# An RMSNorm and swish kernel: row loads and stores regrouped, the first stores held back, and some row sums moved to ScalarE

## The chip, the cores and the metric

The kernel runs on one core of one Trainium2 chip. The metric is the device time of one execution in microseconds (us), as the median of several runs. Slow runs, over 1.5% above the fastest of the same kernel, are left out. A *span* is the stretch that the profile covers in one execution; the time is about 1.3 us longer (160.02 us against 158.7 us in the profiled run of the kernel before). "Row" means a row in each of 128 partitions: 512 floats, 2 KB in a partition, 0.262 MB in all. The kernel moves 128 such rows in and 128 out. A *piece* is the part of one transfer that belongs to one partition: a load of 16 rows has 128 pieces of 32 KB.

## The reference

```python
def reference(x, gamma, eps):            # x: 16 x 1024 x 512 float32
    rms = np.sqrt(np.mean(x ** 2, axis=-1, keepdims=True) + eps)
    x_norm = x / rms * gamma
    return (x_norm * (1.0 / (1.0 + np.exp(-x_norm)))).astype(np.float32)
```

## The kernel before

The rows go through the core in 32 units of 4. For unit k, ScalarE squares and sums one row by itself (its accumulator) and squares the other three into PSUM; VectorE sums those three; GpSimd makes 1/rms; VectorE multiplies the four rows by it and by gamma, in place; ScalarE applies the swish, in place. SyncE issues the loads, ScalarE's queue the stores. The buffer is a ring of 96 rows, so the last 32 rows are loaded only when the first 32 have been stored.

```python
    sizes = [4, 4, 8] + [16] * 6 + [8, 8]     # rows of one load, and of one store
    ring = 96
    cn = 4                                    # rows of a unit
    n_sq = 3                                  # rows of a unit that VectorE sums
    ...
    def load(t):
        ...                                   # waits for the stores that free its part of the ring
        return nc.sync.dma_start(out=buf(t), in_=dram(xf, t)).then_inc(ld[t], 16)
    ...
    def square(k):
        t, at, first = chunks[k]
        if first:
            nc.scalar.wait_ge(ld[t], 16)
        acc = nc.scalar.activation(
            out=junk[k % 2], in_=xb[:, at + n_sq, :], func=AF.Square,
            scale=inv_d**0.5, accum_out=ms[:, k, n_sq : n_sq + 1],
        )
        ...
        square = nc.scalar.activation(
            out=sq[k % 2][:, 0:n_sq, :], in_=xb[:, at : at + n_sq, :],
            func=AF.Square, scale=inv_d**0.5,
        )
    ...
    for k in range(K + 3):
        if k < K:
            square(k)
        while stored < T and ends[stored] <= k - 2:
            store(stored)
            stored += 1
        if 2 <= k < K + 2:
            swish(k - 2)
```

Of the kernel before, what the change touches and what calls it, by code (L numbers as in the profile page):

```python
# [8 lines left out]
@with_exitstack  # L9
def kernel(  # L10
    ctx: ExitStack,
    tc: tile.TileContext,
    x: bass.AP,
    gamma: bass.AP,
    eps: bass.AP,
    out: bass.AP,
):
    nc = tc.nc
    P = nc.NUM_PARTITIONS
    AF = mybir.ActivationFunctionType  # L20
    ALU = mybir.AluOpType
    fp32 = mybir.dt.float32
    bf16 = mybir.dt.bfloat16

    xf = x.flatten_outer_dims()
    of = out.flatten_outer_dims()
    R, D = xf.shape


    sizes = [4, 4, 8] + [16] * 6 + [8, 8]  # L30
    ring = 96
    early = 2
    cn = 4
    n_sq = 3
    N = sum(sizes)
    assert N * P == R, (N, R)


    tiles = []
    done = 0  # L40
    for sz in sizes:
        assert done % ring + sz <= ring
        tiles.append((done * P, sz, done % ring))
        done += sz
    T = len(tiles)

    chunks = [
        (t, r, r == at)
        for t, (_, sz, at) in enumerate(tiles)
        for r in range(at, at + sz, cn)  # L50
    ]
    K = len(chunks)
    ends = []
    e = 0
    for sz in sizes:
        e += sz // cn
        ends.append(e)

    inv_d = 1.0 / float(D)
    eps_f = float(eps)  # L60



    tc.close()
    tc.compile()  # L65

    def sbuf(name, shape, dt=fp32):
        return nc.alloc_sbuf_tensor(name, shape, dt).ap()

    xb = sbuf("xb", [P, ring, D])  # L70
    gamma4 = sbuf("gamma4", [P, D])
    gamma_sb = sbuf("gamma_sb", [P, D])
    junk = [sbuf(f"junk{i}", [P, D], bf16) for i in range(2)]
    neg_half = sbuf("neg_half", [P, cn])
    ms = sbuf("ms", [P, K, cn])
    aeps = sbuf("aeps", [P, K, cn])
    rstd = sbuf("rstd", [P, K, cn])
    sq = [nc.alloc_psum_tensor(f"sq{i}", [P, 4, D], fp32).ap() for i in range(2)]

    ld = [nc.alloc_semaphore(f"ld{t}") for t in range(T)]  # L80
    st = [nc.alloc_semaphore(f"st{t}") for t in range(T)]
    scratch = nc.dram_tensor("scratch", [P, 16], fp32, kind="Internal").ap()
    blank = sbuf("blank", [P, 16])
    s_blank = nc.alloc_semaphore("s_blank")
    s_scratch = nc.alloc_semaphore("s_scratch")
    s_gld = nc.alloc_semaphore("s_gld")
    s_zero = nc.alloc_semaphore("s_zero")
    s_half = nc.alloc_semaphore("s_half")
    s_gamma = nc.alloc_semaphore("s_gamma")
    s_acc = nc.alloc_semaphore("s_acc")  # L90
    s_sq = nc.alloc_semaphore("s_sq")
    s_sum = nc.alloc_semaphore("s_sum")
    s_eps = nc.alloc_semaphore("s_eps")
    s_rstd = nc.alloc_semaphore("s_rstd")
    s_norm = nc.alloc_semaphore("s_norm")
    s_swish = nc.alloc_semaphore("s_swish")

    def need(ins, sem, value):
        return ins.wait_op(sem, value, "sem-ge")

    def dram(ap, t):
        first, sz, _ = tiles[t]
        return ap[first : first + P * sz].rearrange("(p n) d -> p n d", n=sz)

    def buf(t):
        _, sz, at = tiles[t]
        return xb[:, at : at + sz, :]


    stored_by_sync = set()  # L110

    def load(t):
        _, sz, at = tiles[t]
        waits = [
            u for u in range(t)
            if tiles[u][2] < at + sz and at < tiles[u][2] + tiles[u][1]
            and u not in stored_by_sync
        ]
        for u in waits:
            nc.sync.wait_ge(st[u], 16)  # L120
            stored_by_sync.add(u)
        return nc.sync.dma_start(out=buf(t), in_=dram(xf, t)).then_inc(ld[t], 16)

    entry = nc.main_func.blocks[0].instructions
    here = nc.cur_bb.bb.instructions
    for t in range(early):
        ins = load(t).ins
        assert here[-1] is ins or here[-1].name == ins.name
        here.pop()
        at = next(  # L130
            i for i, other in enumerate(entry)
            if other.engine == mybir.EngineType.SP
            and isinstance(other, mybir.InstDrain)
        )
        entry.insert(at, ins)
    for t in range(early, T):
        load(t)
    nc.sync.wait_ge(s_scratch, 16)


    nc.gpsimd.memset(blank, 0.0).then_inc(s_blank, 1)  # L141
    nc.gpsimd.memset(gamma4, 0.0).then_inc(s_zero, 1)  # L142
    nc.gpsimd.memset(neg_half, -0.5).then_inc(s_half, 1)  # L143
    nc.gpsimd.wait_ge(s_half, 1)
    for k in range(K):
        need(
            nc.gpsimd.tensor_scalar(  # L147
                out=aeps[:, k, :], in0=ms[:, k, :], scalar1=eps_f, scalar2=None,
                op0=ALU.add,
            ),  # L150
            s_sum, k + 1,
        ).then_inc(s_eps, 1)
        need(
            nc.gpsimd.tensor_tensor(  # L154
                out=rstd[:, k, :], in0=aeps[:, k, :], in1=neg_half, op=ALU.pow
            ),
            s_eps, k + 1,
        ).then_inc(s_rstd, 1)


    def square(k):
        t, at, first = chunks[k]
        if first:
            nc.scalar.wait_ge(ld[t], 16)
        acc = nc.scalar.activation(  # L165
            out=junk[k % 2], in_=xb[:, at + n_sq, :], func=AF.Square,
            scale=inv_d**0.5, accum_out=ms[:, k, n_sq : n_sq + 1],
        )
        if k >= 2:
            need(acc, s_acc, k - 1)  # L170
        acc.then_inc(s_acc, 1)
        square = nc.scalar.activation(  # L172
            out=sq[k % 2][:, 0:n_sq, :], in_=xb[:, at : at + n_sq, :],
            func=AF.Square, scale=inv_d**0.5,
        )
        if k >= 2:
            need(square, s_sum, k - 1)
        square.then_inc(s_sq, 1)

    def swish(k):  # L180
        _, at, _ = chunks[k]
        rows = xb[:, at : at + cn, :]
        need(
            nc.scalar.activation(out=rows, in_=rows, func=AF.Silu), s_norm, k + 1  # L184
        ).then_inc(s_swish, 1)

    def store(t):
        need(
            nc.scalar.dma_start(out=dram(of, t), in_=buf(t)), s_swish, ends[t]
        ).then_inc(st[t], 16)  # L190

    need(nc.scalar.dma_start(out=scratch, in_=blank), s_blank, 1).then_inc(
        s_scratch, 16
    )
    need(
        nc.scalar.dma_start(out=gamma4[0:P:32, :], in_=gamma.partition_broadcast(4)),
        s_zero, 1,
    ).then_inc(s_gld, 16)
    nc.scalar.preload_act_table_set("silu_and_others")  # L199
    stored = 0  # L200
    for k in range(K + 3):
        if k < K:
            square(k)
        while stored < T and ends[stored] <= k - 2:
            store(stored)
            stored += 1
        if 2 <= k < K + 2:
            swish(k - 2)


    def sums(k):
        need(
            nc.vector.tensor_reduce(  # L213
                out=ms[:, k, 0:n_sq], in_=sq[k % 2][:, 0:n_sq, :], op=ALU.add,
                axis=mybir.AxisListType.X,
            ),
            s_sq, k + 1,
        ).then_inc(s_sum, 1)

    def norm(k):  # L220
        _, at, _ = chunks[k]
        for j in range(cn):
            row = xb[:, at + j, :]
            ins = nc.vector.scalar_tensor_tensor(  # L224
                out=row, in0=row, scalar=rstd[:, k, j : j + 1], in1=gamma_sb,
                op0=ALU.mult, op1=ALU.mult,
            )
            if j == 0:
                need(ins, s_rstd, k + 1)
        ins.then_inc(s_norm, 1)  # L230

    for k in range(K + 1):
        if k < K:
            sums(k)
        if k == 0:
            need(
                nc.vector.stream_shuffle(gamma_sb, gamma4, [0] * 32), s_gld, 16  # L237
            ).then_inc(s_gamma, 1)
        if k == 1:
            nc.vector.wait_ge(s_gamma, 1)  # L240
        if k >= 1:
            norm(k - 1)


    for t in range(T):
        if t not in stored_by_sync:
            nc.sync.wait_ge(st[t], 16)

# [34 lines left out]
```

## Time and profile before

| | kernel before |
|---|---|
| time | 160.11 us, median of 3 (159.87 to 160.23) |
| busy: VectorE, ScalarE, GpSimd | 87%, 79%, 41% of the span |
| the 16 DMA engines | 99.2% of the span, 67.15 MB, 423 GB/s |
| last store: issued, landed | 150.1 us, 158.7 us |

These lines of the groups (shapes kept apart) are the ones that the change touches; the columns are line, engine, operation, output and input, count, then busy us and mean ns of one, then the idle time before them:

```profile
L213 DVE TENSOR_REDUCE ms<-sq 128x3 f32<-128x1536 f32 x32 | 56.1, 1754 | 7.0 <-ACT sq L172 7.0
L172 ACT ACTIVATE sq<-xb 128x1536 f32<-128x1536 f32 x32 | 45.9, 1433 | 0.0
L165 ACT ACTIVATE junk<-xb 128x512 bf16<-128x512 f32 x32 | 19.7, 615 | 3.4 <-DMA xb<-in_x_dram 3.3
```

A row sum on VectorE is at most a third of 1754 ns (585 ns); on ScalarE it is an operation of its own of 615 ns.

### The profile page before, as it was taken

The page shows a single profiled execution, that of the slowest core. Times are in us where ns is not written, and L with a number is a line of the kernel's source. Part 1 is how long each engine was busy: PE and PEld are TensorE (multiplying, and loading weights), DVE is VectorE, ACT ScalarE, POOL GpSimd, SP SyncE. Part 2 cuts the span into 40 slices and gives each one's busy share as a digit, 9 for nine tenths or more (in the row PEclk, how much of TensorE's full clock was granted, in tenths as well). Part 3 has the DMA queues.
Part 4 walks back from the last instruction along what each step waited for, and adds up shares of the span by engine and source line. Part 5 has one row for each costly group of instructions (what it writes and reads, how often), then busy time and mean ns, then how long its engine had stood idle before and what let it go on. Part 6 is the DMA issues. An engine that isn't in the chain of part 4 may idle for free.

```text
span 158.7 us, 439 instructions
## 1 busy us (share of the span) xinstructions
DVE 138.9 (87%) x162; ACT 125.3 (79%) x129; POOL 65.4 (41%) x71
## 2 busy tenths in 40 slices
DVE  0249999999999999999999999999999999999300
ACT  0935989888888889988888888888998888883600
POOL 2035444444455555544444445555544444445000
DMA  7999999999999999999999999999999999999997
GB/s 235 427 523 405 396 450 419 409 452 407 460 394 413 467 421 452 413 396 479 432 413 429 446 429 413 425 417 458 429 454 396 434 446 438 446 413 438 388 458 301
DMA packets 3324, 67.15 MB, mean 423 GB/s; under 512 B 501, under 2 KB 501, under 8 KB 505
## 3 DMA queue, kind: packets, MB, share of 16 engines
q1 hardware_dynamic: 1584, 33.56, 49.9%
q10 hardware_dynamic: 1736, 33.57, 49.3%
q14 instruction: 4, 0.02, 0.0%
HBM read 33.56 MB, written 33.56 MB: 423 GB/s over the span
## 4 chain that ended last, share of the span: by engine, by line
DVE 85%; DMA 5%; ACT 1%; issue 1%; POOL 0%; POOLq 0%
DVE xb L224 53%; DVE ms L213 32%; DMA gamma<-in_gamma_dram 5%; ACT xb L184 1%; DVE gamma_sb L237 0%; POOL gamma L142 0%; POOL blank L141 0%; POOLq L65 0%
## 5 line engine op out<-in xcount | busy, mean ns | idle before, releaser
L224 DVE SCALAR_TENSOR_TENSOR xb<-xb,rstd,gamma_sb 128x512 f32<-128x512 f32 x128 | 87.4, 748 | 0.0
L184 ACT ACTIVATE xb<-xb 128x2048 f32<-128x2048 f32 x32 | 61.1, 1909 | 17.8 <-DVE xb L224 17.8
L213 DVE TENSOR_REDUCE ms<-sq 128x3 f32<-128x1536 f32 x32 | 56.1, 1754 | 7.0 <-ACT sq L172 7.0
L147 POOL TENSOR_SCALAR aeps<-ms 128x4 f32<-128x4 f32 x32 | 20.6, 644 | 75.2 <-DVE ms L213 75.2
L172 ACT ACTIVATE sq<-xb 128x1536 f32<-128x1536 f32 x32 | 45.9, 1433 | 0.0
L154 POOL TENSOR_TENSOR rstd<-aeps,neg_half 128x4 f32<-128x4 f32 x32 | 44.0, 1376 | 2.7
L165 ACT ACTIVATE junk<-xb 128x512 bf16<-128x512 f32 x32 | 19.7, 615 | 3.4 <-DMA xb<-in_x_dram 3.3
L165 ACT ACTIVATION_READ_ACCUMULATOR junk<-xb 128x1 f32 x32 | 6.0, 186 | 0.0
L199 ACT ACT_TABLE_LOAD x1 | 1.3, 1283 | 3.6 <-issue 3.6
L237 DVE LOAD_MASK_SELECT gamma_sb<-gamma x1 | 0.0, 14 | 2.3 <-DMA gamma<-in_gamma_dram 2.3
L141 POOL MEMSET blank<- 128x16 f32 x1 | 0.1, 111 | 1.5 <-POOLq L65 1.5
L237 DVE STREAM_SHUFFLE gamma_sb<-gamma 128x512 f32<-128x512 f32 x1 | 0.7, 717 | 0.0
L142 POOL MEMSET gamma<- 128x512 f32 x1 | 0.5, 524 | 0.0
L264 POOL MEMSET const-float32-0.0<- 128x1 f32 x1 | 0.1, 98 | 0.2 <-issue 0.2
L264 POOL MEMSET const-bfloat16-1.0<- 128x1 bf16 x1 | 0.1, 102 | 0.0
L264 POOL MEMSET const-uint8-127<- 128x1 uint8 x1 | 0.1, 101 | 0.0
L143 POOL MEMSET neg_half<- 128x4 f32 x1 | 0.1, 101 | 0.0
L264 POOL MEMSET const-float32-1.0<- 128x1 f32 x1 | 0.1, 98 | 0.0
## 6 DMA issues: line engine op xcount, KB each, us to landing
xb<-in_x_dram SPq DMA_DIRECT2D x6, 4096.0 KB, 41.9
out_dram<-xb ACTq DMA_DIRECT2D x6, 4096.0 KB, 31.1
xb<-in_x_dram SPq DMA_DIRECT2D x3, 2048.0 KB, 35.0
out_dram<-xb ACTq DMA_DIRECT2D x3, 2048.0 KB, 10.7
xb<-in_x_dram SPq DMA_DIRECT2D x2, 1024.0 KB, 5.8
out_dram<-xb ACTq DMA_DIRECT2D x2, 1024.0 KB, 20.8
scratch<-blank ACTq DMA_DIRECT2D x1, 8.0 KB, 7.7
gamma<-in_gamma_dram ACTq DMA_DIRECT2D x1, 8.0 KB
```

What stands on the lines that cost most here:

```text
L141: nc.gpsimd.memset(blank, 0.0).then_inc(s_blank, 1)
L142: nc.gpsimd.memset(gamma4, 0.0).then_inc(s_zero, 1)
L147: nc.gpsimd.tensor_scalar(out=aeps[:, k, :], in0=ms[:, k, :], scalar1=eps_f, scalar2=None, op0=ALU.add,),
L154: nc.gpsimd.tensor_tensor(out=rstd[:, k, :], in0=aeps[:, k, :], in1=neg_half, op=ALU.pow),
L165: acc = nc.scalar.activation(out=junk[k % 2], in_=xb[:, at + n_sq, :], func=AF.Square, scale=inv_d**0.5, accum_out=ms[:, k, n_sq : n_sq + 1],)
L172: square = nc.scalar.activation(out=sq[k % 2][:, 0:n_sq, :], in_=xb[:, at : at + n_sq, :], func=AF.Square, scale=inv_d**0.5,)
L184: nc.scalar.activation(out=rows, in_=rows, func=AF.Silu), s_norm, k + 1
L199: nc.scalar.preload_act_table_set("silu_and_others")
L213: nc.vector.tensor_reduce(out=ms[:, k, 0:n_sq], in_=sq[k % 2][:, 0:n_sq, :], op=ALU.add, axis=mybir.AxisListType.X,),
L224: ins = nc.vector.scalar_tensor_tensor(out=row, in0=row, scalar=rstd[:, k, j : j + 1], in1=gamma_sb, op0=ALU.mult, op1=ALU.mult,)
L237: nc.vector.stream_shuffle(gamma_sb, gamma4, [0] * 32), s_gld, 16
L264: nc = _bacc.Bacc("TRN2", target_bir_lowering=False, num_devices=1)
```

## The change

The intent: take load off VectorE, and order the transfers so that loads run ahead before stores begin. One load and one store have pieces of 64 KB (32 rows), the first two stores have 8 rows, no store is issued before unit 8, and every third unit has two row sums on ScalarE in place of one. The core of the diff:

```diff
-    sizes = [4, 4, 8] + [16] * 6 + [8, 8]
+    groups = [16, 16, 16, 48, 16, 16]
+    # (group, first row in it, rows)
+    loads = [(0, 0, 4), (0, 4, 4), (0, 8, 8), (1, 0, 16), (2, 0, 16), (3, 0, 16),
+        (3, 16, 32), (4, 0, 16), (5, 0, 16)]
+    stores = [(0, 0, 8), (0, 8, 8), (1, 0, 16), (2, 0, 16), (3, 0, 32), (3, 32, 16),
+        (4, 0, 16), (5, 0, 8), (5, 8, 8)]
-    n_sq = 3
+    held = 8
+    def n_sq(k):
+        return 2 if k % 3 == 2 else 3
 ...
-        acc = nc.scalar.activation(
-            out=junk[k % 2], in_=xb[:, at + n_sq, :], func=AF.Square,
-            scale=inv_d**0.5, accum_out=ms[:, k, n_sq : n_sq + 1],
-        )
+        n = n_sq(k)
+        for j in range(n, cn):
+            acc = nc.scalar.activation(
+                out=junk[j % 2], in_=xb[:, at + j, :], func=AF.Square,
+                scale=inv_d**0.5, accum_out=ms[:, k, j : j + 1],
+            )
 ...
-        while stored < T and ends[stored] <= k - 2:
+        while k >= held and stored < len(stores) and ends[stored] <= k - 2:
```

One more thing changes, in lines cut above: the transfers of a group read and write DRAM through the layout of the whole group. In the kernel before, the pieces of a transfer lie one after the other in DRAM. In the changed kernel the pieces of the group of 48 rows begin 96 KB apart (48 x 2 KB), those of the 4- and 8-row transfers 32 KB apart.

More of the change, by code (lines that the diff above doesn't have):

```diff
@@ L27 @@
     R, D = xf.shape
-    sizes = [4, 4, 8] + [16] * 6 + [8, 8]
+    groups = [16, 16, 16, 48, 16, 16]
+    G = len(groups)
+    assert sum(groups) * P == R, R
+    begin = [sum(groups[:g]) for g in range(G)]
     ring = 96
+    loads = [(0, 0, 4), (0, 4, 4), (0, 8, 8), (1, 0, 16), (2, 0, 16), (3, 0, 16),
+        (3, 16, 32), (4, 0, 16), (5, 0, 16)]
+    stores = [(0, 0, 8), (0, 8, 8), (1, 0, 16), (2, 0, 16), (3, 0, 32), (3, 32, 16),
+        (4, 0, 16), (5, 0, 8), (5, 8, 8)]
     early = 2
     cn = 4
-    n_sq = 3
-    N = sum(sizes)
-    assert N * P == R, (N, R)
-    tiles = []
-    done = 0
-    for sz in sizes:
-        assert done % ring + sz <= ring
-        tiles.append((done * P, sz, done % ring))
-        done += sz
-    T = len(tiles)
-    chunks = [
-        (t, r, r == at)
-        for t, (_, sz, at) in enumerate(tiles)
-        for r in range(at, at + sz, cn)
-    ]
-    K = len(chunks)
-    ends = []
-    e = 0
-    for sz in sizes:
-        e += sz // cn
-        ends.append(e)
+    held = 8
+    def n_sq(k):
+        return 2 if k % 3 == 2 else 3
+    chunks = []
+    new = list(range(len(loads)))
+    for g in range(G):
+        for c in range(0, groups[g], cn):
+            need_now = [
+                i for i in new if loads[i][0] == g and loads[i][1] < c + cn
+            ]
+            new = [i for i in new if i not in need_now]
+            chunks.append(((begin[g] + c) % ring, need_now))
+    assert not new
+    K = len(chunks)
+    ends = [-(-(begin[g] + r + n) // cn) for g, r, n in stores]
     inv_d = 1.0 / float(D)
@@ L78 @@
     sq = [nc.alloc_psum_tensor(f"sq{i}", [P, 4, D], fp32).ap() for i in range(2)]
-    ld = [nc.alloc_semaphore(f"ld{t}") for t in range(T)]
-    st = [nc.alloc_semaphore(f"st{t}") for t in range(T)]
+    ld = [nc.alloc_semaphore(f"ld{t}") for t in range(len(loads))]
+    st = [nc.alloc_semaphore(f"st{t}") for t in range(len(stores))]
     scratch = nc.dram_tensor("scratch", [P, 16], fp32, kind="Internal").ap()
@@ L89 @@
     s_gamma = nc.alloc_semaphore("s_gamma")
-    s_acc = nc.alloc_semaphore("s_acc")
+    s_acc = [nc.alloc_semaphore(f"s_acc{i}") for i in range(2)]
     s_sq = nc.alloc_semaphore("s_sq")
@@ L99, in need, with dram, buf, load @@
         return ins.wait_op(sem, value, "sem-ge")
-    def dram(ap, t):
-        first, sz, _ = tiles[t]
-        return ap[first : first + P * sz].rearrange("(p n) d -> p n d", n=sz)
-    def buf(t):
-        _, sz, at = tiles[t]
-        return xb[:, at : at + sz, :]
-    stored_by_sync = set()
-    def load(t):
-        _, sz, at = tiles[t]
-        waits = [
-            u for u in range(t)
-            if tiles[u][2] < at + sz and at < tiles[u][2] + tiles[u][1]
-            and u not in stored_by_sync
-        ]
-        for u in waits:
-            nc.sync.wait_ge(st[u], 16)
-            stored_by_sync.add(u)
-        return nc.sync.dma_start(out=buf(t), in_=dram(xf, t)).then_inc(ld[t], 16)
+    def dram(ap, piece):
+        g, r, n = piece
+        rows = ap[begin[g] * P : (begin[g] + groups[g]) * P]
+        return rows.rearrange("(p n) d -> p n d", n=groups[g])[:, r : r + n, :]
+    def buf(piece):
+        g, r, n = piece
+        at = (begin[g] + r) % ring
+        assert at + n <= ring
+        return xb[:, at : at + n, :]
+    stored_by_sync = set()
+    def load(i):
+        g, r, n = loads[i]
+        old = begin[g] + r - ring
+        for u, (h, q, m) in enumerate(stores):
+            if (
+                begin[h] + q < old + n and old < begin[h] + q + m
+                and u not in stored_by_sync
+            ):
+                nc.sync.wait_ge(st[u], 16)
+                stored_by_sync.add(u)
+        return nc.sync.dma_start(
+            out=buf(loads[i]), in_=dram(xf, loads[i])
+        ).then_inc(ld[i], 16)
     entry = nc.main_func.blocks[0].instructions
@@ L135 @@
         entry.insert(at, ins)
-    for t in range(early, T):
+    for t in range(early, len(loads)):
         load(t)
@@ L158 @@
         ).then_inc(s_rstd, 1)
+    acc_on = [0, 0]
     def square(k):
-        t, at, first = chunks[k]
-        if first:
-            nc.scalar.wait_ge(ld[t], 16)
-        acc = nc.scalar.activation(
-            out=junk[k % 2], in_=xb[:, at + n_sq, :], func=AF.Square,
-            scale=inv_d**0.5, accum_out=ms[:, k, n_sq : n_sq + 1],
-        )
-        if k >= 2:
-            need(acc, s_acc, k - 1)
-        acc.then_inc(s_acc, 1)
+        at, landing = chunks[k]
+        for i in landing:
+            nc.scalar.wait_ge(ld[i], 16)
+        n = n_sq(k)
[4 more added lines that the diff above has]
+            )
+            last = acc_on[j % 2]
+            if last:
+                need(acc, s_acc[j % 2], last)
+            acc.then_inc(s_acc[j % 2], 1)
+            acc_on[j % 2] += 1
         square = nc.scalar.activation(
-            out=sq[k % 2][:, 0:n_sq, :], in_=xb[:, at : at + n_sq, :],
+            out=sq[k % 2][:, 0:n, :], in_=xb[:, at : at + n, :],
             func=AF.Square, scale=inv_d**0.5,
@@ L180, in swish @@
     def swish(k):
-        _, at, _ = chunks[k]
+        at, _ = chunks[k]
         rows = xb[:, at : at + cn, :]
@@ L188, in store @@
         need(
-            nc.scalar.dma_start(out=dram(of, t), in_=buf(t)), s_swish, ends[t]
+            nc.scalar.dma_start(out=dram(of, stores[t]), in_=buf(stores[t])),
+            s_swish, ends[t],
         ).then_inc(st[t], 16)
@@ L213, in sums @@
             nc.vector.tensor_reduce(
-                out=ms[:, k, 0:n_sq], in_=sq[k % 2][:, 0:n_sq, :], op=ALU.add,
+                out=ms[:, k, 0 : n_sq(k)], in_=sq[k % 2][:, 0 : n_sq(k), :], op=ALU.add,
                 axis=mybir.AxisListType.X,
@@ L220, in norm @@
     def norm(k):
-        _, at, _ = chunks[k]
+        at, _ = chunks[k]
         for j in range(cn):
@@ L242 @@
             norm(k - 1)
-    for t in range(T):
+    for t in range(len(stores)):
         if t not in stored_by_sync:
```

## The prediction

> **What bounds the kernel now.** I read the page from the top, then the windows, then the chain of waits from its end, then single transfers. Rows of busy time first: VectorE looks like the bound, ScalarE close behind.
>
> ```profile
> span 158.7 us, 439 instructions
> DVE 138.9 (87%) x162; ACT 125.3 (79%) x129; POOL 65.4 (41%) x71
> DMA  7999999999999999999999999999999999999997
> q1 hardware_dynamic: 1584, 33.56, 49.9%
> q10 hardware_dynamic: 1736, 33.57, 49.3%
> ```
>
> The reader is to see the DMA row. Only the first and the last of 40 slices are below nine tenths, and the load queue (q1) and the store queue (q10) together took 99.2% of 16 engines' span. The windows (length, busy time of the three engines, clock, DMA share, GB/s) say the same in the steady part:
>
> ```profile
> 24.00:130.00 106.00, 106.00 (x124) 94.85 (x98) 49.32 (x50) 1.00 1.00 431
> 132.00:157.50 25.50, 16.14 (x20) 13.58 (x12) 6.25 (x7) 1.00 0.99 427
> ```
>
> In the first, both VectorE (106 of 106) and the DMA engines (share 1.00) are full, so the averages cannot choose. The second can: VectorE does 16.14 us of 25.50, the DMA goes on at 0.99. The end of the chain and of the timeline settles it:
>
> ```profile
> 142.84 5.31 DVE xb L224 x8
> 148.17 1.91 ACT xb L184
> 143.15 0.34 ACTq L189 DMA_DIRECT2D out_dram<-xb  x1
> 150.11 0.34 ACTq L189 DMA_DIRECT2D out_dram<-xb  x1
> ```
>
> The last two lines are the issues of the last two stores, of 8 rows each ("rows" below means rows in each partition, of 2 KB; 128 x 2 KB = 0.262 MB, and the kernel moves 128 rows in and 128 out). By the view of single transfers the one of 143.15 took 10.7 us to land, so it landed at 153.8; the one of 150.11 took 8.6 and landed at 158.7. So when the last result was ready, the store queue was still 3.7 us behind with work it already had. The chain names VectorE for 85% of the span, but that follows the last store back to its data; it does not show that the store then stood in a queue. I take the DMA engines as the bound and the compute side as ahead by 3.7 us.
>
> Two more transfers show how loads and stores share the engines:
>
> ```profile
> L189 ACTq DMA_DIRECT2D out_dram<-xb x1: 339/339/339, 22.5 to 22.5; - x1
> DMA to landing us min/median/max: 25.0/25.0/25.0
> L122 SPq DMA_DIRECT2D xb<-in_x_dram x1: 569/569/569, 3.3 to 3.3; - x1
> DMA to landing us min/median/max: 44.0/44.0/44.0
> ```
>
> A store of only 4 rows issued at 22.5 landed at 47.5, together with a load of 16 rows (3.3 + 44.0 = 47.3). The next pair, 8 stored rows and 16 loaded ones, ended at 62.0 and 63.1, and the pair of 16 and 16 at 81.3 and 82.4. The queues alternate one piece against one piece, whatever a piece's size, each transfer having one piece per partition: 8 KB pieces of the store against 32 KB pieces of the load. All 112 rows from 63.1 to 130.8 took 67.7 us, so 0.604 us per row, 434 GB/s. The last 32 stored rows (139.4 to 158.7) took 0.603 us each. Mixed or one-way traffic makes no difference here.
>
> **What the Trainium skill says.** "DMA: Bandwidth & Descriptors", section "Where 436 GB/s comes from", puts the ceiling of the 16 engines at 435.2 GB/s. The trace agrees: 434 by landings, 431 by windows. The same page, "Queues, rings and completion order", says that each engine goes round robin between its queues at packet granularity; the three pairs above agree. "ScalarE: Activation LUTs", section "What ACT_TABLE_LOAD costs", gives 186 ns + 0.833 ns per element; the trace has 615 ns for 512 elements and 1433 for 1536, against 613 and 1466. "VectorE: DVE Perf Modes", section "The perf-mode tier table", holds a reduction to one element a cycle, at the page's 0.96 GHz 1600 ns for 1536; the trace has 1754, so about 154 ns are fixed.
>
> **The change part by part.**
>
> *Row sums.* Of 32 units, 10 (every third) reduce two rows on VectorE in place of three. Each such reduction loses 512 elements, an estimated 512 / 0.96 = 533 ns, and falls from 1754 to some 1220; VectorE loses 10 x 0.53 = 5.3 us of its 138.9. ScalarE gets a second row sum of 0.615 us, plus the 0.186 us accumulator read, which overlap by about 0.17 us in the timeline (0.63 us from one start to the square's), and loses 0.43 us of the square: some +0.2 us in each of the 10 units. It idles 0.45 us in a normal unit (its wait for VectorE, 17.8 us over 32 units), so it fits. But the loop norm, swish, next square, reduction is nearly closed: before a reduction the square ends 24.46, the reduction starts 24.59 and VectorE came free about 24.67. So perhaps half of the 5.3 us comes back as small waits. The compute side should end 2.5 to 5 us earlier, near 145 to 147.5 rather than 150.1. As the bound is the DMA, this is worth 0.
>
> *Bytes and rate.* Bytes stay at 67.15 MB. Loads and stores go from 11 + 11 transfers to 9 + 9; at 128 + 16 packets each that is 576 fewer of 3324, or 36 per engine. At 434 GB/s all bytes take 154.7 us of the 158.7; about 1.5 us is the start (76 GB/s in the first 1.5 us) and about 0.7 the end (next to nothing moves after 158.0). That leaves 1.8 us for all gaps and packet costs; a sixth fewer packets can give back perhaps 0.3 us.
>
> *Held stores.* In the kernel before, the first store is issued at 18.0. In the changed one it stands behind the squares of unit 8, whose first one waits for the rows 32 to 48. Loads alone land those at 12.2 + 32 x 0.604 = 31.5 us, and ScalarE gets to unit 8 near 39 (unit 3 at 17.9, then 4.3 each), so the store goes out between 32 and 39; I work with 35. Until then the DMA does loads alone, at the same rate, so nothing is lost: by 35 it has (35 - 2.5) x 1.656 = 54 rows, where 2.5 is 12.2 less 16 rows' time. Then 10 rows of the load of rows 48 to 64 remain (5 pieces of 2 rows), beside 5 store pieces of 1 row. Then the 64 KB load: 8 pieces per engine of 4 rows, against 8 store pieces of 1 row, as the first two stores have 16 KB pieces. It lands at 35 + (10 + 5 + 32 + 8) x 0.604 = 68 us. Unit 16, its first user, is due on ScalarE at about 39 + 8 x 4.2 = 73. So the small first stores are there to let the long load through, with 5 us in hand.
>
> *No hole in the DMA.* The load that reuses the ring needs the first two stores: 3 rows of them are left at 68, so they land near 70, and it is issued then. Meanwhile the third store (issued near 46) keeps the engines busy. Load and store, 16 rows each, end near 70 + 32 x 0.604 = 89; the last load and the fourth store near 109; unit 24 and unit 28 want those loads at about 106 and 123. From 109 on 80 rows of stores are left: 109 + 80 x 0.604 = 157.5, plus the end. Each is issued before its turn: the 64 KB store at about unit 22 (98 us), the rest 16 rows at a time, and the last, of 8 rows, at 145 to 147.5, while its turn comes at 152.6. The slack of compute grows from 3.7 to 5 or more us and the end stays. Sum: 0 for the sums, 0 for the order, -0.3 for packets: 158.4 us of span, and with the 1.3 us by which the time of that run exceeds its span (160.02 - 158.7), 159.7.
>
> **The rivals.** First, VectorE is the bound after all and its relief counts in full: 160.1 - 5.3 = 154.8, or about 157.5 with half of it. For it: 87% busy, 85% of the chain, no idle in the middle. Against it: the store still in the queue at 150.1, and that 67.15 MB at 435 GB/s need 154.3 us, to which the start, the end and the 1.3 outside the span come: 157.8. So even a perfect result is 1.4% faster.
>
> Second, the 64 KB load becomes the new wait. If a 64 KB row is cut into two pieces of 32 KB, the load has 16 pieces per engine and lets as many store pieces through; it then lands after 35 + (15 + 32 + 3 + 8 + 10) x 0.604 = 76 us, and unit 16 waits some 3 us, 2 to 4 by the issue time. The DMA stays busy meanwhile with stores, and compute has 5 us in hand, so 159.7 to 160.5. It costs more only if the engines run out of stores: a wait of over 8 us would be seen, at about one for one.
>
> Third, holding the stores leaves the engines empty somewhere: between the landing of the 96th row and the issue of the ring's next load only stores feed them. If the third store came late, a hole of some 2 us would cost 2 us: 161.7. Against it: it is issued 20 us before.
>
> Fourth, long pieces are moved better or worse than short ones. A ceiling at 434 of 435 leaves no room up; were 64 KB pieces 5% slower, 64 of 256 rows would cost 64 x 0.604 x 0.05 = 1.9 us: 161.6. Nothing in the trace shows any 64 KB piece.
>
> **Range and chances.** Predicted 159.7 us. The lower end, 158.5, is all but 0.7 us of the gap to the ceiling; the upper, 161.3, holds a late load or a small hole. Faster by over 2% means below 156.9, under the computed floor of 157.8: 2%. Slower by over 2% means above 163.3, which takes two of the rivals at once or an idle I did not see: 4%. Within 2%: 94%.
>
> **What would show it.** Right: the DMA row again nine from second to last slice but one, the steady windows at 428 to 436 GB/s, VectorE busy 133 to 134 us, reductions of two rows at some 1.22 us, x10; idle time of VectorE up by 1 to 3 us; the first store issued at 32 to 39 and the 64 KB load landed near 68; the last store issued 2.5 us or more earlier and taking that much longer to land. Wrong: the last store's time to landing still near 8.6 us with an earlier issue (compute was the bound), a ScalarE wait of several us for a load near 70 us, a DMA slice of 8 or less in the middle, or a steady rate off 431 by over 2%.

## The result

| | before | changed |
|---|---|---|
| time | 160.17 us (159.87 to 160.28, 4 runs) | 161.11 us (160.82 to 161.20, 4 runs) |
| ratio | | 1.0058, 95% interval 1.0039 to 1.0078 |
| span of the profiled run | 158.7 us | 159.7 us |

A ratio here is the mean time of one kernel's fast runs over that of the other's in the same rounds, so not quite the ratio of the medians. The change is 0.6% slower: within 2%, within the predicted range, but on the other side of the kernel before than I had forecast. The page of the changed kernel, the lines that answer to those of before:

```profile
span 159.7 us, 453 instructions
DVE 134.4 (84%) x162; ACT 126.4 (79%) x149; POOL 65.5 (41%) x71
DMA  7999999999989989699999999999999979999996
q1 hardware_dynamic: 1296, 33.56, 50.1%
q10 hardware_dynamic: 1448, 33.57, 48.8%
```

VectorE is relieved of 4.5 us and the span is 1.0 us longer. The windows of the changed kernel (length, busy VectorE, ScalarE, GpSimd, clock, DMA share, GB/s):

```profile
24.00:130.00 106.00, 104.83 (x127) 97.89 (x119) 51.15 (x50) 1.00 1.00 425
132.00:157.50 25.50, 12.81 (x17) 11.07 (x10) 5.10 (x5) 1.00 0.99 426
```

The DMA share is 1.00 as before, but in the steady stretch the same engines, as busy, move 425 GB/s in place of 431. In its second half nothing has changed (426 against 427). The end of the changed kernel's timeline (start, us, engine, line; "ACTq" lines are the issues of the last two stores), and the transfer view of the last store and of the 64 KB load:

```profile
139.58 5.38 DVE L241 SCALAR_TENSOR_TENSOR xb<-xb,rstd,gamma_sb 128x512 f32<-128x512 f32 x8
139.97 0.34 ACTq L205 DMA_DIRECT2D out_dram<-xb  x1
146.93 0.34 ACTq L205 DMA_DIRECT2D out_dram<-xb  x1
```

```profile
L205 ACTq DMA_DIRECT2D out_dram<-xb x1: 338/338/338, 146.9 to 146.9; - x1
DMA to landing us min/median/max: 12.7/12.7/12.7
L130 SPq DMA_DIRECT2D xb<-in_x_dram x1: 474/474/474, 3.9 to 3.9; - x1
DMA to landing us min/median/max: 64.1/64.1/64.1
```

The last store is issued 3.2 us earlier and takes 4.1 us longer to land: compute runs further ahead, and the end does not follow it. The 64 KB load, issued at 3.9, landed at 68.0, where the prediction had put it (in part by luck, as shown below).

**Where the rate is lost.** The windows by stage, first of the kernel before, then of the changed one:

```profile
34.00:46.00 12.00, 12.00 (x15) 10.92 (x12) 6.13 (x6) 1.00 1.02 427
80.00:100.00 20.00, 20.00 (x24) 17.73 (x19) 8.73 (x10) 1.00 1.01 434
```

```profile
34.00:46.00 12.00, 11.86 (x16) 11.04 (x15) 6.14 (x6) 1.00 1.00 385
80.00:100.00 20.00, 19.71 (x26) 18.44 (x22) 10.23 (x10) 1.00 0.99 419
```

Two places lose: the stretch after the first stores are issued (37.05 us), and one near 85 us. A window counts whole packets, so these rates are rough; the trace's record of each DMA packet (one packet is one partition's piece of a transfer) is exact. In both kernels a packet nearly always takes the same time for its size: 309 ns for 8 KB, 611 for 16, 1213 for 32, 2418 for 64 (medians). Some take longer. Here are some of the changed kernel's packets, as start and end in us, queue (q1 loads, q10 stores), bytes and ns:

```
36.81-38.03 q1 32768 took 1213
38.14-39.96 q1 32768 took 1813
39.28-41.58 q1 32768 took 2304
41.11-44.21 q1 65536 took 3101
41.28-41.89 q10 16384 took 611
42.66-45.50 q1 65536 took 2846
```

The stores were issued at 37.05 and 37.43. Their first packet starts at 41.28, but from 38.0 on the load packets are stretched, up to 2304 ns in place of 1213, and so are the first packets of the 64 KB load. Store packets keep their 611 ns. I call *stretch* the time by which packets exceed the median of their size. Adding up all packets of both queues, as a mean over the 16 engines, gives this budget of the end of the span, in us:

| | before | changed | change |
|---|---|---|---|
| first packet of an engine (mean) | 1.18 | 1.25 | +0.07 |
| all packets at the median time of their size | 155.98 | 155.69 | -0.29 |
| stretch in the first 5 us | 0.72 | 0.45 | -0.27 |
| stretch after that | 0.70 | 1.77 | +1.07 |
| gaps, overlaps, last receipts (the rest of the sum) | -0.29 | -0.18 | +0.11 |
| mean landing of the last store over the engines | 158.29 | 158.99 | |
| the last engine behind that mean | 0.37 | 0.69 | +0.32 |
| end | 158.66 | 159.68 | +1.02 |

The engines are never empty: counting packets in flight, they idle 0.03 us per engine between 2 and 158 us in the changed kernel, 0.18 before. So no hole was made, no wait was added on the end's path; some load packets became slower (one profiled execution of each kernel), and the slowest engine, not the mean one, sets the end. The experiments ask which part of the change does this.

### The profile page after: what moved, and what is told of

The parts are those of the page before. It is cut to its first block, busy times and chain, and to the rows that moved or that the text cites. A ratio compares the mean times of both kernels' runs of the same rounds, so it can differ in the third digit from the quotient of the medians.

```text
span 159.7 us, 453 instructions
## 1 busy us (share of the span) xinstructions
DVE 134.4 (84%) x162; ACT 126.4 (79%) x149; POOL 65.5 (41%) x71
## 4 chain that ended last, share of the span: by engine, by line
DVE 59%; ACT 23%; DMA 5%; issue 4%; POOL 0%; POOLq 0%
DVE xb L241 37%; DVE ms L230 21%; ACT xb L200 11%; ACT sq L188 8%; DMA gamma<-in_gamma_dram 5%; ACT junk L179 4%; DVE gamma_sb L254 0%; POOL gamma L152 0%; POOL blank L151 0%; POOLq L70 0%
## 5 line engine op out<-in xcount | busy, mean ns | idle before, releaser
L230 DVE TENSOR_REDUCE ms<-sq 128x3 f32<-128x1536 f32 (+1 forms) x32 | 50.8, 1587 | 8.5 <-ACT sq L188 7.0
L188 ACT ACTIVATE sq<-xb 128x1536 f32<-128x1536 f32 (+1 forms) x32 | 41.6, 1299 | 0.0
L179 ACT ACTIVATE junk<-xb 128x512 bf16<-128x512 f32 x42 | 25.8, 614 | 3.4 <-DMA xb<-in_x_dram 3.4
L179 ACT ACTIVATION_READ_ACCUMULATOR junk<-xb 128x1 f32 x42 | 7.8, 186 | 0.0
```

The costliest lines, as they stand in the source:

```text
L179: acc = nc.scalar.activation(out=junk[j % 2], in_=xb[:, at + j, :], func=AF.Square, scale=inv_d**0.5, accum_out=ms[:, k, j : j + 1],)
L188: square = nc.scalar.activation(out=sq[k % 2][:, 0:n, :], in_=xb[:, at : at + n, :], func=AF.Square, scale=inv_d**0.5,)
L230: nc.vector.tensor_reduce(out=ms[:, k, 0 : n_sq(k)], in_=sq[k % 2][:, 0 : n_sq(k), :], op=ALU.add, axis=mybir.AxisListType.X,),
```

## The experiments

All were correct, and timed in 5 rounds beside the kernel before, whose median was 160.07 to 160.09 us; the first two lines of the table are from the result above. The profiled runs were all fast, but for before_hold; each is one execution, not always one at the median (store_split's took 161.98 us). "Stretch" is from each profiled run, for the times 5 to 70 us (first stores) and 70 to 100 us (after the loads have paused and begun again); "lag" is the last engine behind the mean landing of the last store. The 160.52 us of before_hold is the median of all six runs, of which one was slow; its ratio is of the fast ones.

| run | us | ratio to before, 95% | stretch 5-70 | stretch 70-100 | lag |
|---|---|---|---|---|---|
| kernel before | 160.17 | | 0.57 | 0.09 | 0.37 |
| changed kernel | 161.11 | 1.0058 (1.0039 to 1.0078) | 1.39 | 0.37 | 0.69 |
| sums_only | 160.21 | 1.0002 (0.9985 to 1.0018) | 0.59 | 0.02 | 0.69 |
| no_hold | 160.61 | 1.0032 (1.0008 to 1.0055) | 0.80 | 0.05 | 0.42 |
| load_split | 160.27 | 1.0011 (0.9998 to 1.0025) | 0.84 | 0.02 | 0.88 |
| before_hold | 160.52 | 1.0043 (1.0004 to 1.0082) | slow profile | | |
| hold_6 | 161.22 | 1.0068 (1.0055 to 1.0081) | 0.62 | 0.50 | 1.37 |
| hold_10 | 162.33 | 1.0142 (1.0127 to 1.0156) | 0.95 | 0.07 | 2.47 |
| stores_4row | 160.73 | 1.0038 (1.0025 to 1.0051) | 0.87 | 0.04 | 0.71 |
| three_sums | 162.21 | 1.0133 (1.0117 to 1.0149) | 0.46 | 0.58 | 2.77 |
| split_three_sums | 160.67 | 1.0065 (1.0023 to 1.0107) | 0.67 | 0.02 | 0.61 |
| store_split | 161.19 | 1.0073 (1.0058 to 1.0089) | 0.79 | 0.87 | 1.59 |
| store_16row | 162.05 | 1.0129 (1.0115 to 1.0144) | 1.13 | 0.66 | 1.65 |
| split_4row | 160.74 | 1.0041 (1.0027 to 1.0056) | 0.56 | 0.94 | 0.48 |

The profiles hold two forms of loss. The mean landing of the last store over the engines is 158.99 us in the changed kernel, and 158.90 to 159.29 in no_hold, store_split, store_16row and split_4row: all engines are late together. In hold_6, hold_10 and three_sums it is 158.29 to 158.39, where the kernel before has 158.29: there nearly the whole loss is lag, one or a few engines behind the rest. In load_split it is 158.12.

### sums_only: the row sums alone

```diff
 (kernel before)
-    n_sq = 3
+    def n_sq(k):
+        return 2 if k % 3 == 2 else 3
 (and the loop over the accumulator sums, as in the change)
```

> The kernel before with only the row sums changed (two on ScalarE in every third unit). My theory (the DMA engines are the bound, the sums only make slack): time within 0.3 us of the kernel before, last store issued 2 to 4 us earlier and landing at the same time. Rival (VectorE is the bound after all): 3 to 5 us faster. Second rival (the sums are what cost the 0.94 us): 161.1 us.

Measured 160.21 us, ratio 1.0002. The last store went out 2.8 us earlier than before (150.11):

```profile
147.28 0.34 ACTq L198 DMA_DIRECT2D out_dram<-xb  x1
```

It landed at 158.9. VectorE was relieved and nothing was gained: it is not the bound, and the sums by themselves cost nothing.

### no_hold: stores allowed at once

```diff
-    held = 8
+    held = 0
```

> The changed kernel with stores allowed at once. Theory (the 0.94 us are lost where the store queue starts late, with two stores of 16 KB pieces, in the middle of the loads: load packets there are stretched, 1.4 us per engine in the profile of the changed kernel): most of it comes back, 160.2 to 160.6 us, stretched load packets at the first store 0.7 us or less. Rival (the 64 KB load's own packets are slow): stays at 161.0 or above, and the 64 KB packets take 2.9 us again.

Measured 160.61 us, in two groups of runs (160.12 to 160.26, and 160.96 to 161.18). The number is at the edge of what I expected, but the reason is mixed. The profiled run took 161.07 us, so it belongs to the upper group, and what follows is shown for that group only. Stretch fell to 0.80 us and the packets of the 64 KB load were not slow (10 ns over the median on average), so 64 KB packets are not slow whenever they come. In its place a new wait appears. The waits, and the transfer view of the two last loads of the first batch:

```profile
ACT junk L179 <- DMA xb<-in_x_dram: 9.9, 4, 6.6
L130 SPq DMA_DIRECT2D xb<-in_x_dram x2: 449/545/641, 3.2 to 3.9; - x2
DMA to landing us min/median/max: 47.3/61.0/74.7
```

The 64 KB load (the later, issued at 3.9) lands at 78.6 and ScalarE waits 6.6 us for it. Compute falls behind: the last store goes out at 153.08 and the engines stand empty for 1.06 us, at 138 to 140 and at 152 to 154. This is what the hold is for: it lets the long load through before it is wanted.

### load_split: the 64 KB load as two of 32 KB

```diff
-        (3, 16, 32), (4, 0, 16), (5, 0, 16)]
+        (3, 16, 16), (3, 32, 16), (4, 0, 16), (5, 0, 16)]
```

> The changed kernel with its 64 KB load cut into two loads of 32 KB rows. Theory of the late start of the stores: still 160.8 to 161.3 us, as the stores start as late and as the first one is stretched before any 64 KB packet. Rival of the 64 KB load: back to about 160.2 to 160.5 us, as the first 64 KB packets took 0.5 us longer than later ones.

Measured 160.27 us, ratio 1.0011 with an interval that holds 1 and lies below that of the changed kernel. My theory of the late start falls in that form and the rival stands: some 0.75 of the 0.94 us come back with this one cut. Its windows:

```profile
34.00:46.00 12.00, 11.85 (x16) 11.04 (x15) 6.13 (x6) 1.00 0.99 404
80.00:100.00 20.00, 19.71 (x26) 18.36 (x22) 10.22 (x10) 1.00 1.02 439
```

Between 34 and 46 us it moves 404 GB/s, half way between 385 and 427, and near 85 us the loss is gone. The store still starts at the same time (first packet at 41.1), and stretches the load packet in front of it by some 0.6 us; what is missing is the second part, on the first 64 KB packets.

This run also bears on the layout in DRAM: load_split keeps that of the changed kernel and still gets most of the time back. In the changed kernel's trace the load that was stretched first (rows 48 to 64, pieces 96 KB apart) had run since 29.9 us with 96 packets at 1213 or 1214 ns before the stretch began. So the layout by itself does not stretch packets. Whether it has a part in the stretch that came with the stores is not tested.

### before_hold: the hold alone

```diff
 (kernel before)
-        while stored < T and ends[stored] <= k - 2:
+        while k >= 8 and stored < T and ends[stored] <= k - 2:
```

> The kernel before with only the hold (no store before unit 8; its first stores have pieces of 8, 8 and 16 KB). Theory of the late start: 0.4 to 1.0 us slower than the kernel before, and stretched load packets at 37 to 45 us. Rival of the 64 KB load, or of the sums: the same as the kernel before within 0.3 us.

Inconclusive. The median of the five fast runs, 160.50 us, is 0.43 us above the kernel before, at the lower edge of what the theory had, but the interval reaches from nothing to 0.8%: four of the five lie at 160.31 to 160.55, one at 162.41. The profiled run was a slow one (163.33 us), so its packets say nothing here.

### hold_6 and hold_10: the first stores 8 us earlier, or 8 us later

```diff
-    held = 8
+    held = 6        (hold_10: 10)
```

> The changed kernel with the stores held until unit 6 in place of 8: both first stores go out near 30 us, while loads of 32 KB rows still have some 18 rows to go, and the 64 KB load begins near 47 with stores already flowing. Theory (the loss is the start of the stores meeting the start of the 64 KB load): 0.5 to 0.8 us faster than the changed kernel, 160.3 to 160.6, stretched load packets near 31 to 36 us of 0.6 to 0.8 us per engine and nothing in the first 64 KB packets. Rival (64 KB packets beside stores are slow whenever they come, or the loss is in the 64 KB store): 161.0. The 64 KB load should land near 72, just before unit 16 wants it.

> The changed kernel with the stores held until unit 10: the first stores go out near 46 us, in the middle of the 64 KB load. Theory that the start of stores costs about one store piece's time (0.6 us for 16 KB) unless it falls on the change from 32 to 64 KB pieces: 160.3 to 160.6 us. Theory that a start beside 64 KB pieces costs double or more wherever it falls: 160.9 to 161.4, with stretched 64 KB packets near 46 to 52 us of 1.2 us per engine or more.

hold_6 gave 161.22 us where I expected 160.3 to 160.6. The first 64 KB packets were indeed not stretched, and the first stores cost 0.55 us per engine as foreseen, but 0.46 us came back at 84 to 88 us, and the lag rose to 1.37. hold_10 gave 162.33, more than either theory. Its mean stretch is not larger than that of hold_6; its lag is: a few engines fell far behind. So the theory "the start of the stores on the edge of the 64 KB load" falls too.

### stores_4row and store_16row: smaller and larger first stores

```diff
-    stores = [(0, 0, 8), (0, 8, 8), ...
+    stores = [(0, 0, 4), (0, 4, 4), (0, 8, 4), (0, 12, 4), ...     (stores_4row)
+    stores = [(0, 0, 16), ...                                      (store_16row)
```

> The changed kernel with its first two stores of 8 rows cut into four of 4 rows (8 KB pieces). Theory that the loss goes with the size of the first store pieces: stretched packets at 37 to 46 us fall from 1.3 us per engine to 0.7 or less, time 160.4 to 160.8. Rival (size plays no part): 161.1.

> The changed kernel with its first two stores as one of 16 rows (32 KB pieces), beside the 64 KB load. Theory that the stretch grows with the first store's pieces (8 KB pieces gave 160.7, 16 KB 161.1): 161.3 to 162.5 us. Theory that unequal pieces are the trouble (64 beside 16): 160.7 or less. By the count of pieces the 64 KB load lands near 76 and unit 16 waits for it some 3 us, which the slack should hold.

With the 64 KB load in place, first pieces of 8, 16 and 32 KB gave 160.73, 161.11 and 162.05 us: in order, and both new ones inside what the theory of size gave. Store_16row also had 0.66 us of stretch after 70 us. Its last store was out at 147.7, so it was not starved. By the count of pieces the 64 KB load was to land near 76; it landed at 73.2, and ScalarE waited 1.2 us for it in place of some 3.

### three_sums and split_three_sums: the row sums undone

```diff
-        return 2 if k % 3 == 2 else 3
+        return 3        (split_three_sums: with the 64 KB load cut as well)
```

> The changed kernel with three rows on VectorE in every unit, as before. Theory (DMA engines are the bound): 160.9 to 161.3 us, the last store issued 2 to 4 us later, landing at the same time. Rival (the sums have to do with the loss, or give something back): off 161.1 by 0.4 us or more.

> The changed kernel with the 64 KB load cut in two and three rows on VectorE in every unit. Cutting the load alone gave 160.27, three rows alone 162.2. Theory (the sums cost or give nothing themselves; with the 64 KB load in place they only moved the first store by 0.6 us, from the edge of that load into it): 160.1 to 160.5 us. Rival (the sums are worth about 1.1 us to the held order whatever the loads are): 161.2 or more.

three_sums was the surprise: 162.21 us, 1.1 above the changed kernel, though VectorE's work is not the bound. Its last store was issued at 149.9 and landed at 161.15, so it queued for 11 us: compute was not late. The trace does not name a packet's engine, but in this profile the packets can be joined end to start into 16 chains of about 4.19 MB each, with next to no gaps. As far as this joining goes, 13 of them had 0.5 to 1.4 us of stretch after 5 us, two had about 2, and one had 3.6 to 3.8; the end follows that one. Its first store packet starts at 43.0, inside the 64 KB load, in the changed kernel at 41.28, at its edge; the store was issued 0.6 us later (37.63), as VectorE had more to do.

split_three_sums is unclear. Its six runs lie between 159.96 and 162.14 us; two of them are in the range that I expected, one is below it, three are above. It does say that a run with a late start of the stores, no 64 KB load and three sums can be as fast as the kernel before (159.96 us), and also that without the 64 KB load the time can still scatter. That the sums are worth nothing in themselves rests on sums_only.

### store_split: the 64 KB store as two of 32 KB

```diff
-        (3, 0, 32), (3, 32, 16),
+        (3, 0, 16), (3, 16, 16), (3, 32, 16),
```

> The changed kernel with only its 64 KB store cut in two. Theory (the loss is the 64 KB load; the 64 KB store runs when no loads are left): 160.8 to 161.4 us, the same as the changed kernel. Rival (64 KB pieces cost in either direction): 160.5 or less.

Measured 161.19 us, the same as the changed kernel. The 64 KB store is not needed for the loss.

### split_4row: both findings together

```diff
 (the 64 KB load cut as in load_split, the first stores cut as in stores_4row)
```

> The changed kernel with the 64 KB load cut in two and the first two stores cut into four of 4 rows: the version that both findings point to. Theory: stretched load packets at the first store fall from 0.6 us per engine to 0.3 or less, time 159.7 to 160.1, 0 to 0.3 us under the kernel before. Rival (the remaining loss has nothing to do with the first pieces' size): 160.2 to 160.4 as with the load cut alone.

Measured 160.74 us, where I expected 159.7 to 160.1. The stretch at the first stores did fall (0.30 us at 36 to 44), but 0.90 us appeared at 80 to 88, where load_split had next to none. The two findings do not add up, and no version beats the kernel before.

## Why the prediction was right or wrong

**The bound: right.** The DMA engines set the end. VectorE lost 4.5 us of busy time, the last store went out 3.2 us earlier, and both the changed kernel and sums_only end where the queue lets them. The first rival (VectorE counts in full, 154.8) is excluded by sums_only.

**Row sums: right, term by term.** The groups of the changed kernel:

```profile
L230 DVE TENSOR_REDUCE ms<-sq 128x3 f32<-128x1536 f32 x22 | 38.6, 1754 | 8.5 <-ACT sq L188 7.0
L230 DVE TENSOR_REDUCE ms<-sq 128x2 f32<-128x1024 f32 x10 | 12.2, 1218 | 0.0
```

A reduction of two rows takes 1218 ns (predicted some 1220), and all reductions together lost 56.1 - 50.8 = 5.3 us, as predicted; VectorE's busy time fell by 4.5 only, to 134.4 (predicted 133 to 134). VectorE's idle time in the steady window rose by 1.2 us (predicted 1 to 3), as the loop through ScalarE closed.

**Packets: right.** 577 fewer, and 0.29 us less of packet time (predicted 0.3).

**Held stores: the step that was off.** The order was right: first store at 37.05 us (32 to 39), the 64 KB load at 68.0 (68), no wait for it, no hole. That 68.0 agrees is in part luck. The sum let store pieces flow from the issue on, but the first one ran at 41.28, 4.2 us after it, so fewer of them came between the load's pieces than counted. The stretch, and 1.4 us from the load's last packet (66.6) to its landing, made up for it. The step said that until the first store "the DMA does loads alone, at the same rate, so nothing is lost", and that mixed or one-way traffic makes no difference. That holds within each phase. What I gave no term is the passage from one to the other: when stores begin beside loads in flight, load packets stretch. Stretch after the first 5 us went from 0.70 to 1.77 us, +1.07, against 0 in the sum; the lag of the last engine added 0.32. The predicted 159.7 missed by 1.4 us and on the wrong side of the kernel before. That the time stayed within the range is luck: its upper end, 161.3, was meant for a late load or a small hole, and neither cost anything here. The trace of the kernel before already held it in small: 0.20 us at 20 to 24 us, where its first store begins, and 0.31 at 44 to 48, where its stores go from 8 to 16 KB pieces. I had read only rates over long windows, in which it drowns.

**No hole: right, with wrong times.** The load into the ring's first part landed at 96.2 and the last at 120.4 (predicted 89 and 109). After its pause the load queue came in later than I had counted: issued at 72.3, first packet at 75.8. The last load also ran beside the 64 KB store from 107.6, where the fourth store had landed, and the sum had not counted those pieces. Unit 28 wanted the last load at about 123, and the waits of the changed kernel show none for it. One sum on the way was written wrong: 109 + 80 x 0.604 is 157.3, not 157.5. This changes nothing, as the forecast was built on the span before.

**The signs.** Two of my own signs came out against me. The steady rate was 425 GB/s, outside 428 to 436, though not off by 2%. And the DMA row has slices of 8, 8 and 6 between 44 and 68 us and a 7 at 128 to 132. These are no holes: a slice counts a packet whole where it starts, and the 64 KB packets, 2.4 us long in slices of 4 us, run there. Counted in flight, the engines idle 0.03 us. The sign was badly chosen for such packets.

**The rivals.** The second (the 64 KB load becomes a wait) was not this kernel's fate, but it is that of no_hold's profiled run. The fourth had the nearest sign: it gave 161.6 for 64 KB pieces 5% slower. But the pieces are not slow as such (10 ns over the median on average in no_hold); the first of them are slow when stores start beside them.

**What is shown and what is open.** Shown for the changed kernel: the lost time is stretched load packets, on engines that are never empty; cutting the 64 KB load gives most of it back, cutting the 64 KB store or undoing the sums does not; larger first stores beside that load cost more. Open: why a load packet stretches. That the engine fetches store data while the load packet waits would fit a stretch that begins 3 us before the first store packet, but no run tests it. Open too is when the second place, near 85 us, appears: load_split is free of it and split_4row is not, and they differ only in the first stores. And open is what makes single engines fall behind, which is nearly the whole loss of hold_6, hold_10 and three_sums. My rules from size and from position each failed once.

## What to carry to other kernels

When the DMA engines are full from end to end, freeing a compute engine gives nothing, and reordering transfers can give little and lose more: add up what the bytes need and see how much is left before tuning. Look at the packets, not only at the rates: compare each with the median of its size, and look at the last engine as well as the mean, since the end waits for the slowest of the 16. A load with large pieces takes bandwidth from stores with small ones, as the queues alternate piece by piece; that is a way to steer them, but the change from one mix to another has its own cost, here about 1 us.

## What the Trainium skill lacked or had wrong

- "DMA: Bandwidth & Descriptors", on arbitration: it describes round robin between queues, but not that the share of bandwidth then follows the size of the pieces. Here a 64 KB load beside 16 KB stores landed at 68.0 us, as counted by pieces, and at 78.6 in no_hold, where stores had begun earlier and 32 KB store pieces ran beside it.
- No page that I read has the stretch of load packets when stores start: 1213 ns becomes up to 2304, from about 1 us after the issue of the store and 3 us before its first packet.
- The same page, "Latency and other measured facts", lists two engines as usually slower and calls this specific to descriptors written by software. Both queues here are of the hardware kind, and 16 about equally loaded engines still end apart: the last store of the kernel before landed over 0.76 us from the first engine to the last, that of three_sums over 3.4 us.
- "SBUF — State Buffer", section "Summary: rules for kernel authors", advises 358 GB/s as the estimate for transfers between HBM and SBUF. This kernel, alone on its core, has 423 GB/s over the whole span and 431 in the steady part, with loads and stores together.
